# Three half-size raw weight tiles instead of one, and layer 1's embedding projection computed first

## The chip, the cores and the metric

One core of a Trainium2 chip runs the whole program in one launch. The metric is device microseconds of an execution, median of several. Five engines work side by side, each through its own queue in order: TensorE (PE in the profile; its weight loads are PEld), VectorE (DVE), ScalarE (ACT), GpSimd (POOL) and SyncE (SP), which here only issues DMAs.

## The reference, cut to what matters

Two layers on a residual stream of 512 tokens by 1024 columns, float32, then a final RMSNorm:

```python
for i in range(2):
    hn = rmsnorm(x, norm_g[i])
    x = x + (ab_mixer if i == 0 else fox_mixer)(hn, ...)      # hn @ w_in, heads, gate, @ w_out
    gate = sigmoid(rmsnorm(x, ple_norm_g[i]) @ w_ple_gate[i])
    x = x + gate * (p[i] @ w_ple_proj[i])                     # the per-layer embedding
return rmsnorm(x, final_g)
```

Layer 0's mixer has four gated-delta-rule heads (a short convolution on q, k, v; chunks of 64 tokens; a triangular inverse for each chunk) and four block-attention heads. Layer 1's mixer has eight heads with a forget gate (FoX). `p[i] @ w_ple_proj[i]` needs nothing of the residual stream: only `p` (512 by 256) and its weights (256 by 1024).

## The kernel before, in words

**Products.** A float32 product is made of three float32r products: each operand is split into a high part (its value rounded to float32r) and a low part (what is left), and high x high, low x high and high x low are summed in PSUM. One output tile of 128 x 512 (a "unit", `u` in the trace, or four rows of tokens, `vr`) takes 8 x 3 = 24 matmuls with 512 columns each.

**Weights.** Every weight matrix passes through one path (class `Weights`, lines 447 to 533). It is cut into pieces of 1024 x 512 (2 MB); a piece is loaded from DRAM into the tile `raw` (16 KB in each partition; there is one such tile) by two DMAs of 1 MB, one for each half of the rows. A piece is split in four chunks: a copy to `whi` (ACT, or DVE) and a subtraction to `wlo` (POOL, or DVE), each 128 x 1024; there are three `whi` and three `wlo` tiles. A chunk of a "cols" piece feeds one unit and holds all 8 row blocks, so it reads both halves of the piece; a chunk of a "rows" piece holds two row blocks, so it reads one half. `raw` is free for the next piece when the piece's fourth chunk is split. Of 23 pieces 19 are cols, 4 rows; two more chunks are `w_ple_proj[1]`.

**Order.** The order on every engine is written while the program is built, by the class `Plan` (lines 123 to 322). Each strand of work is a Python generator with a priority; `Plan` keeps an estimated time for each engine, tile and the DMA path (`bw`, line 177), and emits an instruction once its estimate says that its inputs are there at the present estimated time of PE. What is emitted is fixed: on the chip each engine runs its list in order and waits for the real event, however late it is. Where the estimate has nothing for PE for 0.2 us or more and a PSUM bank is free, it emits a matmul on a tile of ones, `idle` (line 296): a filler with no result.

**Tiles.** SBUF is cut by hand into pools: `t2` (2 KB tiles of 128 x 512, 55 of them: `NB2`), `t4` (4 KB, four), `raw`, `whi`, `wlo`, and the pair `bd` (8 KB each), which holds first `w_ple_proj[0]` and the gate weights, later the inverted blocks of the delta rule. PSUM banks are pools A (unit results) and B (all else).

**Around the change.** At the start `p[0]`, `w_ple_proj[0]` and `x` are loaded, layer 0's embedding product is computed (`ple_cols`, 48 matmuls, `pp`) and stored to DRAM (`ppd`), `x` is transposed and normalised, and the units of the delta rule's k follow, then the gate unit, q, the block attention's q, k, v, and v. The triangular inverse goes through DRAM (`xd`), from which 8 DMAs place 32 x 32 blocks in `bd` (lines 1182 to 1186); loads of `raw` are held from near the inverse's end until these are issued (line 484). `wy` (line 1188) multiplies with them (`t` in the trace). Layer 1's embedding product stands after the z units of FoX (lines 1588 to 1601), stays in eight `t2` tiles and is used in the last stage (`gate_row`, line 1662).

Of the kernel before, what the change touches and what calls it, by code (L numbers as in the profile page):

```python
# [122 lines left out]
class Plan:  # L123
# [34 lines left out]
    def emit(self, op):  # L158
# [12 lines left out]
        if op.eng == "PE":  # L171
            end += 0.18
        elif op.name == "dma_start":
            o = op.outs[0] if op.outs[0].space != bass.MemoryType.DRAM else op.ins[0]
            b = o.nbytes if not callable(o.nbytes) else o.nbytes()
            small = any(n.startswith(("kd", "ub", "xd", "graw", "vrow", "bd_", "qd", "gd", "Gb")) for n in op.w + op.r)
            self.bw = max(end + 0.7, self.bw) + max(b / 1e6 * 2.8, 0.6 if small else 0.2) + 1.5 * ("graw" in op.w[0])
            end = self.bw + 0.9
# [146 lines left out]
NB2, NBH = 55, 16  # L325
# [4 lines left out]
def kernel(  # L330
# [65 lines left out]
    bd = [gp.tile([P, GH * NT * P], F32, name=nm("bd"), tag="bd", bufs=2)]  # L396
    ple0 = bd[0].rearrange("p (k c) -> p k c", k=2)
    do(A.preload_act_table_set(LNEXP))
    for c in range(2):
        do(A.dma_start(ple0[:, :, c * 512:(c + 1) * 512],  # L400
                       w_ple_proj[0, :, c * 512:(c + 1) * 512].rearrange("(k q) c -> q k c", q=P)))
    do(A.dma_start(vrow1, norm_g.rearrange("i (f q) -> (i f) q", q=P)))
    xr = [plan.take("t4", "xr", (P, D)) for _ in range(NT)]
    for t in range(NT):
        for c in range(2):
            w = slice(c * S, (c + 1) * S)
            do(SP.dma_start(xr[t][:, w], x[0, t * P:(t + 1) * P, w]))
    do(A.dma_start(vrow[17:65], conv_w[0].rearrange("k (f q) -> (k f) q", q=P)))
# [31 lines left out]
    def gst_tile():  # L440
        return gp.tile([P, GH * NT, P], F32R, name=nm("gst"), tag="bd", bufs=2)[:, 0:KT, :]

    gst0 = gst_tile()
# [3 lines left out]
    class Weights:  # L447
# [13 lines left out]
        def cols(self, w, c0):  # L461

            self.add(self.views(w, c0), [(lambda r, j=j: r[:, :, j * P:(j + 1) * P], (KT, P)) for j in range(4)])

        def rows(self, w, c0):

            self.add(self.views(w, c0), [(lambda r, j=j: r[:, 2 * j:2 * j + 2, :], (2, 512)) for j in range(4)])

        def ple(self, w):
            self.add([w[:, c * 512:(c + 1) * 512].rearrange("(k q) c -> q k c", q=P) for c in range(2)],  # L470
                     [(lambda r, c=c: r[:, 2 * c:2 * c + 2, :], (2, 512)) for c in range(2)])
# [6 lines left out]
        def loads(self):  # L478
            for i, views in enumerate(self.pieces):
                if views is None:  # L480
                    self.loaded.append(ple0)
                    continue

                yield Wait(lambda: "inv3" not in flags or "bds" in flags)
                raw = yield Slot("raw", "raw", (P, KT, 512))
                n = views[0].shape[1]
                for k, view in enumerate(views):
                    yield SP.dma_start(raw[:, k * n:(k + 1) * n], view)
                self.loaded.append(raw)

        def splits(self):
            for i, (piece, f, (a, c)) in enumerate(self.chunks):
                yield Wait(lambda: len(self.loaded) > piece)
                raw = f(self.loaded[piece])
# [3 lines left out]
                yield copy(hi, raw, 0.8)  # L498
                w = [V.tensor_tensor(out=lo, in0=raw, in1=hi.bitcast(F32), op=ALU.subtract),
                     G.tensor_tensor(out=lo, in0=raw, in1=hi.bitcast(F32), op=ALU.subtract)]  # L500
                yield Any((w[0], 2.5 if far else 0.0), w[1])
# [34 lines left out]
    W.add(None, [(lambda r, c=c: r[:, :, c * 512:(c + 1) * 512], (2, 512)) for c in range(2)])  # L536
# [18 lines left out]
    W.ple(w_ple_proj[1])  # L555
# [14 lines left out]
    def later_loads():  # L570
        yield Wait(lambda: len(W.loaded) > 1)
# [380 lines left out]
    def spill(f):  # L952
        yield Wait(lambda: pps[f] is not None)
        yield SP.dma_start(ppd[f], pps[f])
        drop(pps[f])
        pps[f] = None
        spilled.add(f)

    ppd = dram.tile([KT, P, S], F32, name="ppd")
    spilled = set()  # L960
# [15 lines left out]

    ple_cols(pps)
    for f in range(KT):
        run(spill(f), 5)
# [176 lines left out]
    def inverses():  # L1156
# [25 lines left out]
        for k in (0, 1):  # L1182
            for bl in range(4):
                yield SP.dma_start(bds[k][bl * 32:(bl + 1) * 32, :, bl * 32:(bl + 1) * 32],
                                   xd[k, bl].rearrange("h t r c -> r (h t) c"))
        flags.add("bds")

    def wy(hh):
# [8 lines left out]
        yield flag("bds")  # L1197
        wq = yield Slot("t4", "wq", (P, NT, 4, 64))
        yield SP.dma_start(wq[:, :, 1:3, :], qd[hh].rearrange("p (t c i) -> p t c i", c=2, i=64))
        bdT, bd = (b[:, hh * NT:(hh + 1) * NT, :] for b in bds)  # L1200
# [28 lines left out]
        us[hh], wqs[hh], kds[hh] = u, wq, kdc  # L1229

# [81 lines left out]
    def blocks():  # L1312
        yield flag("gates")
        for k in range(2):
            bds.append(gp.tile([P, GH * NT, P], F32, name=nm("bd"), tag="bd", bufs=2))
            yield G.memset(bds[k], 0.0)
# [35 lines left out]
    run(gates(gate_unit(st["gst"], h)), -1)  # L1352
    delta()
# [4 lines left out]
    def ev_rows(ps, t, dst, parts, key):  # L1358
# [3 lines left out]
        if parts:  # L1362
            v = (None, t2("vhi", F32R), t2("vlo", F32R))
            yield A.activation(v[1], ps, AF.Copy, scale=s)
            yield V.scalar_tensor_tensor(out=v[2], in0=ps, scalar=s, in1=v[1].bitcast(F32), op0=ALU.mult, op1=ALU.subtract)
        else:
            v = (t2("vb"),)
# [48 lines left out]
    side_units(h, "k", range(4), 1.0, False, qkb)  # L1416
    for t, ps in enumerate(rowsV(h)):
# [9 lines left out]
    run(after(gens, lambda: [v[0] for v in vrows.values()]), 0)  # L1427
# [141 lines left out]
    for half in range(2):  # L1569
# [11 lines left out]
        run(after(gens[4 * half:], lambda half=half: [a for v in vrows2[half].values() for a in v if a is not None]), 0)  # L1581
    pT = []
    run(load_pT(1, None, pT.append, flag("z4")), 4)
# [4 lines left out]
    ppr = [None] * KT  # L1588
    for c in range(2):
        whi, wlo = W.get()  # L1590
        for t in range(NT):
            tt = slice(t * P, (t + 1) * P)
            pp = plan.slot("A", "pp")
            for k in range(2):
                until(lambda: len(pT) > k, "pT")
                for m, (a, b) in enumerate(((pT[k][0], whi), (pT[k][1], whi), (pT[k][0], wlo))):
                    plan.main(T.matmul(pp, lhsT=a[:, tt], rhs=b[:, k], start=(k + m == 0), stop=(k == 1 and m == 2)))
            run(keep(pp, ppr, c * 4 + t), 0)
        W.over((whi, wlo))
    for a in pT:  # L1600
        drop(*a)
# [11 lines left out]
    for a in y:  # L1613
        drop(*a)
    x3, h = x1, h3
# [7 lines left out]
    def late():  # L1623
# [6 lines left out]
        yield Wait(lambda: len(W.loaded) == len(W.pieces))  # L1630
        raw = yield Slot("raw", "raw", (P, KT, 512))
        for kc, view in enumerate(W.views(w_ple_gate[1], 512)):
            yield SP.dma_start(raw[:, kc * 4:(kc + 1) * 4], view)
        for kc in range(2):
            for k in range(4):
# [7 lines left out]
                yield copy(hi, raw[:, kc * 4 + k])  # L1643
                yield minus(lo, raw[:, kc * 4 + k], hi.bitcast(F32), 0.0)
                gw[kc * 4 + k] = (hi, lo)

    run(late(), -0.5)

    def gate_row(t, c, ps, ss, a, b, gt, before=None):
# [10 lines left out]
        if c == 1 and b == 512 and t != 2:  # L1660
            yield A.preload_act_table_set(LNEXP)
        yield V.tensor_tensor(out=gt[:, w], in0=gt[:, w], in1=ppr[c * 4 + t][:, w], op=ALU.mult)
        yield V.tensor_tensor(out=gt[:, w], in0=gt[:, w], in1=xps[:, w], op=ALU.add)
# [104 lines left out]
```

## Time and profile before

| | us |
|---|---|
| median of 3 runs | 742.52 (739.96 to 742.71) |
| the profiled execution | 739.63 |
| its span, first to last instruction | 737.9 |
| PE busy | 702.7 (95%) |
| DVE, ACT, POOL busy | 474.7, 341.1, 279.8 |
| granted TensorE clock, mean | 0.986 of 2.4 GHz |

PE is busy nearly throughout, and the fillers count as busy. What can be saved are the stretches where PE has no work, the fillers in front of them, and the stretches after them in which the clock is at its lower level. The table of 40 slices shows where; windows of a few us show how much.

### The profile page before, as it was taken

Reading aid. Unit: us, or ns where it says so; the run is one execution under the profiler, and the core shown is the slowest. Engines: PE = TensorE matmul, PEld = TensorE weight load, DVE = VectorE, ACT = ScalarE, POOL = GpSimd, SP = SyncE. Lnnn points to the kernel's source line nnn. Section 1 sums busy time; section 2 is a strip of 40 time slices with the busy share of each in tenths; the row PEclk is TensorE's granted clock in tenths of the full one; section 3 lists DMA queues with packets and bytes.
Section 4 is the critical chain, followed back from the end, with each engine's and each line's share of the span. In section 5 each row is a group of like instructions: output and inputs, shape, how many; then the busy total and the mean of one; then the engine's idle time right before and its main releaser. Section 6 shows DMA issues by size and latency. Waiting matters only on the chain.

```text
span 737.9 us, 9199 instructions
## 1 busy us (share of the span) xinstructions
PE 702.7 (95%) x3374; PEld 577.9 (78%) x3374; DVE 474.7 (64%) x805; ACT 341.1 (46%) x634; POOL 279.8 (38%) x222
## 2 busy tenths in 40 slices
PE   7999988999999999999998999989999799999995
PEld 4887876888788787778886888868888688888884
DVE  3768864966665678776896443546337466776684
ACT  4638842225774364634553422345224463433545
POOL 3435554426551223025322344342336322535320
PEclk9999999999999999999999999989999999999998
DMA  7752424443424023143554035310453203244303
GB/s 257 261 144 78 152 73 128 143 114 90 111 58 115 2 69 116 25 165 125 200 185 125 17 116 141 96 49 1 114 143 100 72 1 138 79 170 157 114 1 114
DMA packets 51782, 80.41 MB, mean 109 GB/s; under 512 B 11133, under 2 KB 14542, under 8 KB 51738
## 3 DMA queue, kind: packets, MB, share of 16 engines
q1 hardware_dynamic: 51064, 78.74, 34.5%
q10 hardware_dynamic: 674, 1.09, 0.5%
q8 instruction: 26, 0.43, 0.2%
q14 instruction: 18, 0.15, 0.1%
HBM read 68.53 MB, written 11.30 MB: 108 GB/s over the span
## 4 chain that ended last, share of the span: by engine, by line
PE 69%; DMA 13%; DVE 9%; ACT 3%; POOL 3%; issue 2%; SPq 1%; ACTq 0%; DVEq 0%; POOLq 0%
PE u L186 40%; PE vr L186 8%; DMA raw<-in_w_in_c_dram 6%; DMA raw<-in_w_in_ab_dram 4%; PE O L186 3%; PE pp L186 3%; PE fg L186 3%; POOL wlo L186 2%; PE S L186 2%; ACT whi L186 2%; PE PTp L186 2%; DVE gt L186 1%; DVE wlo L186 1%; DMA bd<-in_w_ple_proj_dram 1%; PE su L186 1%
## 5 line engine op out<-in xcount | busy, mean ns | idle before, releaser
L186 POOL TENSOR_TENSOR wlo<-raw,whi 128x1024 fp32r<-128x1024 f32 x74 | 186.5, 2526 | 360.0 <-ACT whi L186 280.6
L186 PE MATMUL u<-hhi,whi 128*128 128x512 f32 x480 | 190.7, 397 | 3.2 <-ACT whi L186 3.1
L186 PE MATMUL u<-hlo,whi 128*128 128x512 f32 x480 | 190.2, 396 | 0.0
L186 PE MATMUL u<-hhi,wlo 128*128 128x512 f32 x480 | 163.1, 397 | 0.1
L186 ACT ACTIVATE whi<-raw 128x1024 fp32r<-128x1024 f32 x84 | 87.3, 1054 | 117.7 <-DMA raw<-in_w_in_c_dram 49.5
L186 PEld LDWEIGHTS u<-hhi,whi 128*128 128x128 f32 x480 | 90.3, 188 | 22.1 <-ACT whi L186 3.5
L186 PEld LDWEIGHTS u<-hhi,wlo 128*128 128x128 f32 x480 | 89.7, 188 | 18.4 <-POOL wlo L186 0.6
L186 PEld LDWEIGHTS u<-hlo,whi 128*128 128x128 f32 x480 | 90.3, 188 | 17.3
L186 DVE TENSOR_TENSOR wlo<-raw,whi 128x1024 fp32r<-128x1024 f32 x20 | 36.9, 1844 | 24.8 <-ACT whi L186 24.8
L186 PE MATMUL u<-yhi,whi 128*128 128x512 f32 x128 | 50.2, 392 | 1.4 <-ACT whi L186 1.4
L186 PE MATMUL vr<-wlo,hhi 128*128 128x512 f32 x128 | 51.4, 401 | 0.0
L186 PE MATMUL vr<-whi,hlo 128*128 128x512 f32 x128 | 51.3, 401 | 0.0
L186 PE MATMUL vr<-whi,hhi 128*128 128x512 f32 x128 | 51.3, 401 | 0.0
L186 PE MATMUL u<-ylo,whi 128*128 128x512 f32 x128 | 50.0, 391 | 0.0
L186 ACT ACT_TABLE_LOAD x33 | 42.3, 1283 | 2.1 <-DVE cacc L186 0.8
L186 PE MATMUL u<-yhi,wlo 128*128 128x512 f32 x128 | 42.4, 391 | 0.7 <-POOL wlo L186 0.7
L186 ACT ACTIVATE hhi<-xres,vec 128x512 fp32r<-128x512 f32 x24 | 17.3, 724 | 44.1 <-DVE xres L186 44.0
L186 ACT ACTIVATE P<-P,nmx 128x128 f32<-128x128 f32 (+3 forms) x48 | 26.7, 557 | 12.6 <-DVE nmx L186 11.7
L186 DVE SCALAR_TENSOR_TENSOR cacc<-u,vec,cacc 128x509 f32<-128x509 f32 (+2 forms) x36 | 26.7, 744 | 7.0 <-ACT cacc L186 6.4
L186 PEld LDWEIGHTS u<-yhi,whi 128*128 128x128 f32 x128 | 24.1, 188 | 6.7 <-ACT whi L186 1.9
L186 PEld LDWEIGHTS u<-yhi,wlo 128*128 128x128 f32 x128 | 24.0, 188 | 6.0 <-POOL wlo L186 1.1
L186 PEld LDWEIGHTS vr<-whi,hlo 128*128 128x128 f32 x128 | 24.6, 193 | 4.9
(299 smaller groups left out, 1277.8 us busy)
## 6 DMA issues: line engine op xcount, KB each, us to landing
raw<-in_w_in_ab_dram SPq DMA_DIRECT2D x16, 1024.0 KB, 9.7
raw<-in_w_in_c_dram SPq DMA_DIRECT2D x16, 1024.0 KB, 7.0
raw<-in_w_ple_gate_dram SPq DMA_DIRECT2D x8, 1024.0 KB, 5.0
raw<-in_w_out_ab_dram SPq DMA_DIRECT2D x4, 1024.0 KB, 7.2
raw<-in_w_out_c_dram SPq DMA_DIRECT2D x4, 1024.0 KB, 6.5
xr<-in_x_dram SPq DMA_DIRECT2D x8, 256.0 KB, 5.6
x0d<-x SPq DMA_DIRECT2D x8, 256.0 KB, 8.0
ppd<-ppt SPq DMA_DIRECT2D x8, 256.0 KB, 4.1
```

The costliest lines, as they stand in the source:

```text
L186: return op.f(*op.a, **op.k)
```

## The change

- `raw` becomes three tiles of 8 KB, each for half a piece. A half is loaded as soon as one of the three is free. A chunk of a cols piece is split from its two halves by two copies and two subtractions of 128 x 512 each; a chunk of a rows piece still takes one of each, 128 x 1024.
- `Plan` counts 5.2 us for a MB of the two `w_in` matrices and 3.4 for other data, where it counted 2.8 for all.
- `t4` has 8 tiles, `t2` 51. The pair `bd` is gone: `w_ple_proj[0]`, the gate weights and the inverted blocks lie in `t4` tiles, the blocks in four (two heads each), filled by 16 DMAs of half the size. The values v of the block attention and the split v of FoX move from `t2` to `t4`.
- Layer 1's embedding product is computed right behind layer 0's (`ple_rows`), stored to DRAM (`ppd1`) and loaded back, eight tiles, in the last stage.

```diff
-            self.bw = max(end + 0.7, self.bw) + max(b / 1e6 * 2.8, 0.6 if small else 0.2) + ...
+            self.bw = max(end + 0.7, self.bw) + max(b / 1e6 * (5.2 if any("w_in" in n for n in op.r) else 3.4), 0.6 if small else 0.2) + ...
-NB2, NBH = 55, 16
+NB2, NBH = 51, 16
-    for pool, n in (("A", 4), ("B", 4), ("t2", NB2), ("th", NBH), ("t4", 4),
-                    ("raw", 1), ("whi", 3), ("wlo", 3)):
+    for pool, n in (("A", 4), ("B", 4), ("t2", NB2), ("th", NBH), ("t4", 8),
+                    ("raw", 3), ("whi", 3), ("wlo", 3)):
...
-                raw = yield Slot("raw", "raw", (P, KT, 512))
-                for k, view in enumerate(views):
-                    yield SP.dma_start(raw[:, k * n:(k + 1) * n], view)
-                self.loaded.append(raw)
+                for view in views:
+                    yield Wait(lambda: "inv3" not in flags or "bds" in flags)
+                    raw = yield Slot("raw", "raw", (P, 4, 512))
+                    yield SP.dma_start(raw[:, 0:view.shape[1]], view)
+                    self.loaded[i].append(raw)
...
-                yield copy(hi, raw, 0.8)
+                for h, k, w, o in parts:
+                    yield copy(hi[:, o, :], halves[h][:, k, w], 0.8)
+                for h, k, w, o in parts:
+                    ops = [e.tensor_tensor(out=lo[:, o, :], in0=halves[h][:, k, w], in1=hi[:, o, :].bitcast(F32),
+                                           op=ALU.subtract) for e in (V, G)]
+                    yield Any((ops[0], 2.5 if far else 0.0), ops[1])
...
-                if piece and (i + 1 == len(self.chunks) or self.chunks[i + 1][0] != piece):
-                    free(raw)
+                rest = {x[0] for q in self.chunks[i + 1:] if q[0] == piece for x in q[1]}
+                for h in {x[0] for x in parts} - rest:
+                    free(halves[h])
...
+    W.ple(w_ple_proj[1])          # now second in the list of pieces
...
     ple_cols(pps)
     for f in range(KT):
-        run(spill(f), 5)
+        run(spill(pps, f, ppd), 5)
+    ple_rows()
+    for f in range(KT):
+        run(spill(ppr, f, ppd1), 5)
...
-        for k in (0, 1):
-            for bl in range(4):
-                yield SP.dma_start(bds[k][...], xd[k, bl].rearrange("h t r c -> r (h t) c"))
+        for h0 in range(2):
+            yield Wait(lambda: len(bds) >= 2 * h0 + 2)
+            for k in (0, 1):
+                for bl in range(4):
+                    yield SP.dma_start(bds[2 * h0 + k][...], xd[k, bl, 2 * h0:2 * h0 + 2].rearrange("h t r c -> r (h t) c"))
+            flags.add(f"bds{h0}")
...
-    run(load_pT(1, None, pT.append, flag("z4")), 4)
...
+    for n in range(KT):
+        run(again(n), 3)          # ppr[n] back from ppd1
```

Because `Plan` writes the order anew, instructions move on every engine. Three places matter below.

ACT, in the first attentions of FoX: `whi` is a weight chunk, `PThi` the high part of transposed weights of attention that PE multiplies with v (`O`) next. Before:

```order
L186 ACTIVATE P_4084,sums_4024<-P_4084,nmx_4023 128x512
L186 ACTIVATE P_4092,sums_4063<-P_4092,nmx_4062 128x384
L186 ACTIVATE P_4060<-P_4060,rs_4096 128x384
L186 ACTIVATE whi_4101<-raw_4039 128x1024
L186 ACTIVATE P_4111,sums_4063<-P_4111,nmx_4062 128x512
L186 ACTIVATE PThi_4144<-PTp_4140 128x384
```

and in the change:

```order
L186 ACTIVATE whi_4317<-raw_4119 128x512
L186 ACTIVATE P_4306,sums_4274<-P_4306,nmx_4273 128x384
L186 ACTIVATE P_4316,sums_4298<-P_4316,nmx_4297 128x256
L186 ACTIVATE whi_4317<-raw_4189 128x512
L186 ACTIVATE P_4330,sums_4274<-P_4330,nmx_4273 128x512
L186 ACTIVATE P_4337,sums_4298<-P_4337,nmx_4297 128x384
L186 ACTIVATE P_4306<-P_4306,rs_4345 128x384
L186 ACTIVATE P_4360,sums_4298<-P_4360,nmx_4297 128x512
L186 ACTIVATE whi_4386<-raw_4119 128x512
L186 ACTIVATE PThi_4399<-PTp_4395 128x384
```

The copy of the next piece's first chunk stood two rows above the first `PThi`; it now stands in two parts nine and six rows above it, and the copy just above `PThi` reads a half that an earlier row has read already.

SP, at the end of the triangular inverse: `raw` are the weight loads, `xd` the inverse on its way through DRAM, `bd` its blocks, `wq` a load for the scan. Before:

```order
L186 DMA xd<-vb_650 64x1024
L186 DMA raw_1633<-in_w_in_ab_dram 128x4x512 x2
L186 DMA xd<-vbT_1602 64x1024
L186 DMA bd_1062<-xd 32x16x32 x4
L186 DMA bd_1064<-xd 32x16x32 x4
L186 DMA wq_1741<-qd 128x4x128
```

and in the change:

```order
L186 DMA raw_1784<-in_w_in_ab_dram 128x4x512
L186 DMA xd<-vb_761 64x1024
L186 DMA xd<-vbT_1793 64x1024
L186 DMA bd_1583<-xd 32x8x32 x4
L186 DMA bd_1585<-xd 32x8x32 x4
L186 DMA bd_1815<-xd 32x8x32 x4
L186 DMA bd_1817<-xd 32x8x32 x4
L186 DMA wq_1896<-qd 128x4x128
```

A load of 2 MB that stood between the two stores is now 1 MB ahead of them; eight block loads became sixteen, of which the first eight serve heads 0 and 1.

PE, between the k units of the delta rule with the gate unit (`tr` are transposes of k) and the q units. In the change:

```order
L186 MATMUL tr_791<-ident,cacc_737 128x128 x4
L186 MATMUL idle_812<-onesr 128x512
L186 MATMUL idle_816<-onesr 128x512
L186 MATMUL idle_822<-onesr 128x512
L186 MATMUL idle_824<-onesr 128x512
L186 MATMUL idle_826<-onesr 128x512
L186 MATMUL idle_828<-onesr 128x512
L186 MATMUL idle_831<-onesr 128x512
L186 MATMUL idle_834<-onesr 128x512
L186 MATMUL idle_836<-onesr 128x512
L186 MATMUL u_842<-hhi_373,whi_674 128x512
```

Before, there is no filler at this place; nine of them stand at another, between the fourth and the fifth unit of layer 0's output projection, where the change has none.

## Rows read from the trace of the kernel before

**Rows 1.** The page: busy time of PE; GB/s in 40 slices

```profile
PE 702.7 (95%) x3374; PEld 577.9 (78%) x3374; DVE 474.7 (64%) x805; ACT 341.1 (46%) x634; POOL 279.8 (38%) x222
...
GB/s 257 261 144 78 152 73 128 143 114 90 111 58 115 2 69 116 25 165 125 200 185 125 17 116 141 96 49 1 114 143 100 72 1 138 79 170 157 114 1 114
```

**Rows 2.** Windows: length, PE, PEld, DVE, ACT, POOL busy (x), clock, DMA, GB/s

```profile
92.00:100.00 8.00, 5.15 (x37) 4.68 (x36) 7.62 (x16) 4.69 (x10) 7.74 (x11) 1.00 0.05 8
116.00:122.00 6.00, 2.92 (x13) 2.10 (x12) 1.63 (x2) 2.12 (x3) 0.98 (x1) 1.00 0.55 189
294.00:300.00 6.00, 5.34 (x23) 4.06 (x23) 5.96 (x9) 5.96 (x10) 2.20 (x1) 1.00 0.00 0
314.00:322.00 8.00, 6.56 (x29) 5.07 (x28) 6.13 (x9) 3.68 (x4) 1.35 (x1) 1.00 0.67 252
390.00:400.00 10.00, 6.93 (x24) 5.17 (x23) 7.46 (x9) 4.90 (x6) 4.11 (x2) 0.83 0.11 32
480.00:492.00 12.00, 8.43 (x34) 6.83 (x33) 4.28 (x8) 3.91 (x9) 6.51 (x11) 0.72 0.27 69
566.00:582.00 16.00, 11.74 (x55) 9.54 (x54) 7.00 (x19) 6.16 (x15) 6.13 (x10) 0.89 0.50 157
```

**Rows 3.** Windows of the fillers alone: length, PE and PEld busy, clock

```profile
116.00:122.00 6.00, 0.86 (x3) 0.56 (x3) 1.00 0.55 189
294.00:300.00 6.00, 1.17 (x3) 0.56 (x3) 1.00 0.00 0
314.00:322.00 8.00, 2.23 (x9) 1.69 (x9) 1.00 0.67 252
566.00:582.00 16.00, 2.02 (x6) 1.13 (x6) 0.89 0.50 157
```

**Rows 4.** ACT in order of time: start, length, instruction [idle before <-releaser]

```profile
483.39 1.06 ACT L186 ACTIVATE whi<-raw 128x1024 fp32r<-128x1024 f32 x1 [7.09 <-DMA raw<-in_w_in_c_dram]
...
485.18 0.77 ACT L186 ACTIVATE PThi<-PTp 128x384 fp32r<-128x384 f32 x2
...
574.74 1.06 ACT L186 ACTIVATE whi<-raw 128x1024 fp32r<-128x1024 f32 x1 [5.22 <-DMA raw<-in_w_in_c_dram]
```

**Rows 5.** PE in order of time, in the first of these places

```profile
485.72 0.69 PE L186 MATMUL O<-PThi,vhi 128*128 128x384 f32 x1 [3.57 <-ACT PThi L186]
```

**Rows 6.** The chain that ended last: start, length, what

```profile
45.53 9.94 DMA raw<-in_w_in_ab_dram
...
417.66 43.52 PE u L186 x192
...
469.58 13.65 DMA raw<-in_w_in_c_dram
...
624.96 10.88 PE pp L186 x48
```

**Rows 7.** Instructions on raw: duration ns min/median/max; DMAs to landing

```profile
L186 ACT ACTIVATE whi<-raw x84: 1042/1053/1077, 26.9 to 678.5; 128x1024 fp32r<-128x1024 f32 x84
L186 POOL TENSOR_TENSOR wlo<-raw,whi x74: 2355/2402/3383, 28.0 to 685.5; 128x1024 fp32r<-128x1024 f32 x74
...
L186 ACT ACTIVATE gwhi<-raw x6: 616/618/634, 693.2 to 697.5; 128x512 fp32r<-128x512 f32 x6
...
L186 POOL TENSOR_TENSOR gwlo<-raw,gwhi x2: 1423/1581/1739, 697.1 to 698.5; 128x512 fp32r<-128x512 f32 x2
...
DMA to landing us min/median/max: 4.8/7.2/11.2
```

**Rows 8.** SP's issues in order of time, end of the inverse

```profile
177.84 0.51 SPq L186 DMA_DIRECT2D xd<-vbT  x1
178.45 12.94 SPq L186 DMA_DIRECT2D bd<-xd  x8
```

**Rows 9.** Instructions on bd: duration ns, first and last start us

```profile
L186 PE MATMUL t<-bd,kn x32: 271/275/276, 196.0 to 229.1; 128*128 128x128 f32 x32
```

**Rows 10.** PE in order of time, first matmul of the gate unit

```profile
54.70 0.39 PE L186 MATMUL gate<-hhi,gst 128*128 128x512 f32 x1
```

More of the change, by code (lines that the diff above doesn't have):

```diff
@@ L570, in later_loads @@
     def later_loads():
-        yield Wait(lambda: len(W.loaded) > 1)
+        yield Wait(lambda: len(W.loaded) > 1 and len(W.loaded[1]) == 2)
         yield load_gate("ab", w_in_ab[0], 1536)
@@ L975, in ple_cols, with spill, ple_rows @@
             drop(*a)
+    ppr = [None] * KT
+    ppd1 = dram.tile([KT, P, S], F32, name="ppd1")
+    def spill(dst, f, d):
+        yield Wait(lambda: dst[f] is not None)
+        yield SP.dma_start(d[f], dst[f])
+        drop(dst[f])
+        dst[f] = None
+    def ple_rows():
+        for c in range(2):
+            whi, wlo = W.get()
+            for t in range(NT):
+                tt = slice(t * P, (t + 1) * P)
+                pp = plan.slot("A", "pp")
+                for k in range(2):
+                    until(lambda: len(pT1) > k, "pT")
+                    for m, (a, b) in enumerate(((pT1[k][0], whi), (pT1[k][1], whi), (pT1[k][0], wlo))):
+                        plan.main(T.matmul(pp, lhsT=a[:, tt], rhs=b[:, k], start=(k + m == 0), stop=(k == 1 and m == 2)))
+                run(keep(pp, ppr, c * 4 + t), 0)
+            W.over((whi, wlo))
+        for a in pT1:
+            drop(*a)
+    pT1 = []
+    run(load_pT(1, prow1, pT1.append), -1)
     ple_cols(pps)
     for f in range(KT):
-        run(spill(f), 5)
+        run(spill(pps, f, ppd), 5)
+    ple_rows()
+    for f in range(KT):
+        run(spill(ppr, f, ppd1), 5)
     flags.add("pp")
@@ L1425, in after @@
         drop(*tiles())
-    run(after(gens, lambda: [v[0] for v in vrows.values()]), 0)
+    run(after(gens, lambda: vpair), 0)
     def gating(zs, order, oT, y, g):
@@ L1580 @@
         attend(qk, heads, lambda hh, i: (vrows2[hh // 4][i], slice((hh % 4) * P, (hh % 4 + 1) * P)), bias_c, oTc, 0.2, gens)
-        run(after(gens[4 * half:], lambda half=half: [a for v in vrows2[half].values() for a in v if a is not None]), 0)
-    pT = []
-    run(load_pT(1, None, pT.append, flag("z4")), 4)
+        run(after(gens[4 * half:], lambda half=half: [v[-1] for v in vrows2[half].values()]), 0)
     y = [None] * KT
@@ L1587, with again @@
         drop(*a)
[L1588 to L1601, printed above, removed]
+    def again(n):
+        r = yield Slot("t2", "ppr")
+        yield SP.dma_start(r, ppd1[n])
+        ppr[n] = r
     h3 = [None] * KT
@@ L1629, in late @@
             fg.append(fgt)
[L1630 to L1633, printed above, removed]
+        yield Wait(lambda: len(W.loaded) == len(W.pieces) and len(W.loaded[-1]) == 2)
+        raws = []
+        for view in W.views(w_ple_gate[1], 512):
+            raw = yield Slot("raw", "raw", (P, 4, 512))
+            yield SP.dma_start(raw, view)
+            raws.append(raw)
         for kc in range(2):
```

81 lines of the change are left out of this document (42 added, 39 removed).

## The prediction

> **What bounds the kernel now.** I read the page first: PE is busy 702.7 of 737.9 us [rows 1], so only time in which PE has nothing to do, or does fillers, can be saved. Next the windows around the holes in PE's work: idle time is a window's length less its PE time [rows 2], and the fillers in it are wasted too [rows 3]. The holes inside the run:
>
> | stretch | idle | fillers | together |
> |---|---|---|---|
> | 92 to 100 | 2.85 | 0 | 2.85 |
> | 116 to 122 | 3.08 | 0.86 | 3.94 |
> | 294 to 300 | 0.66 | 1.17 | 1.83 |
> | 314 to 322 | 1.44 | 2.23 | 3.67 |
> | 390 to 400 | 3.07 | 0 | 3.07 |
> | 480 to 492 | 3.57 | 0 | 3.57 |
> | 566 to 582 | 4.26 | 2.02 | 6.28 |
>
> In the window from 480 the mean granted clock is 0.72 [rows 2], so 0.56 of its 12 us, 6.7 us, ran at the lower level (1.2 GHz); 3.57 of these were the idle time, and the other 3.1 did half their work: 1.5 us more lost.
>
> Then I asked what ended the two FoX holes. ACT stood still for 7.09 us in front of a weight copy whose DMA had not landed, and for 5.22 us in front of another; the `PThi` that PE wanted came out right behind the first [rows 4], and PE's wait of 3.57 us ends there [rows 5]. The matmul and its operands were not late: a weight copy that nobody needed yet stood in front of them in ACT's list. The chain of waits names the loads: 9.94 us for a pair of w_in halves in layer 0, 13.65 us for one in layer 1 [rows 6]. The order was written with 2.8 us for a MB, 5.9 us for such a pair (2.1 million bytes). So the holes are late weight loads, seen directly at a unit or through an engine that waits for one in order.
>
> How late they must be: a unit costs 24 x 43.52/192 = 5.44 us [rows 6]. When a piece's fourth chunk is split, three chunks are left, 16.3 us, less the split of the fourth itself, 1.05 + 2.40 [rows 7]: 12.9 us. The next first chunk needs 0.94 for two issues, 9.94 for the pair, and 3.45 for its split: 14.3. Layer 0 is 1.4 us short, layer 1 5.1; pieces that land faster are not.
>
> **The change part by part.** *Three half tiles.* The first half of the next piece is now loaded ahead; only the second waits for the fourth split. A split made of halves takes 2 x 0.618 on ACT and 2 x 1.50 on POOL (middle of 1.42 and 1.58, the two forms of 128 x 512 [rows 7]), 4.2 us instead of 3.45. So 16.3 - 4.2 = 12.1 us are left, and 0.47 + half of 9.94 + 4.2 = 9.6 are needed, or 0.47 + half of 13.65 + 4.2 = 11.5: 2.5 and 0.6 us to spare. A rows piece gives back its first half two chunks earlier still. The four holes at weights (116, 294, 314, 566) go, as does the one from 480, where the ACT list now has the second half of the first chunk six rows above `PThi`: 3.94 + 1.83 + 3.67 + 6.28 + 3.57 + 1.5 = 20.8 us. The hole from 92 is a wait for `kn`, at the end of a chain on DVE; weight copies stand in DVE's list too, but no row says how much of it is load, 0 to 2.85, and I take 1.4. Together 22.2. The hole from 390 is the chain of sums behind the gated residual on a DVE busy 7.46 of 10 us; the change leaves it: 0.
>
> *What the new order puts in their place.* The list of PE has 47 fillers instead of 50: 13 before the first real product of the start (16 before), 4 around the two embedding products (5 in the first units before), 5 near the end (5), and within the run 9, 6, 3 and 7 (24 before). The nine at 314 cost 3.67 us, 0.41 each [rows 2, 3]; where the load was later than planned a filler cost more, but that is the part already taken away. 25 x 0.41 = 10.3 us. Two of the 24 before are at a place that I did not count as a gain, so 9.4 are new. Bounds: 25 x 0.23, the bare matmuls, 5.7, and the 1.3 us a filler of the place at 116, 33. The start gains 4 x 0.41 = 1.6.
>
> *Blocks of the inverse.* PE's list now runs into the first product with the blocks behind the v units. From the store of the inverse to that product it took 196.0 - 177.84 = 18.2 us [rows 8, 9], 12.94 of it for issuing eight loads. Only the first eight of sixteen must land, each half as large. If the issue goes by bytes, 6.5 us go, and 11.7 are left; PE has in its list, from the last rows of the inverse to the product, 45 matmuls of 512 columns and the six fillers, 51 x 0.227 = 11.6 us, and some transposes. Then nothing is late. If it goes by count, 18.2 - 11.6 = 6.6 us. I take 1, near the first, since an issue of a block load took 1.6 us where that of the store took 0.51: something that grows with its content sets it.
>
> *The moved product.* 48 matmuls, 10.88 us [rows 6], go from behind the z units to the start: PE pays them in both places, 0. At the start they are cover, since the DMA path there is full (257 and 261 GB/s in the first two slices [rows 1]). Up to the second half of the q weights 15 MB are asked for instead of some 12 (the product's inputs, 1.5, and its stores, 2): 15/0.259 = 58 us. PE was through the gate unit, 16 matmuls or 3.6 us, at 54.7 + 3.6 = 58.3 [rows 10], and now at some 58.3 + 10.9 = 69, so 11 us are to spare; if the rate fell to 200 GB/s the weights would come at 75, 6 us late. At the later place they covered a load; the half tile does that now. The loads back, 2 MB, stand in SP's queue ahead of the last stage and have most of a rows piece, 96 x 0.227 = 21.8 us, for 2.1/0.211 = 10: 0.
>
> *More, smaller instructions.* 0.8 us a cols chunk, hidden where a chunk is ahead; PE meets a chunk that is just being made at one or two places: 1 us. The two POOL rows are from one stage, so 0 to 5. `t2` with four tiles less has its price in the fillers, most of all in the nine before the q units.
>
> Sum: 739.63 - 22.2 + 9.4 - 1.6 + 1 + 1 = 727.2. The profiled execution lies 2.9 below the median, at the low end of the runs; I forecast 728, against the median of 742.5.
>
> **The rivals.** *The waits only move.* For: 25 fillers stand within the run as 24 did, and every estimate in the order was also wrong before. Then of 22.2 us only what is bare DMA lateness beyond the planned waits could go, 22.2 - 24 x 0.41 = 12.4, and as much comes back in other lists: about 740. Against: 2.8 us a MB was off by a factor of 1.7 to 2.3 from the rows, and 5.2 is not.
>
> *Block loads by count.* 6.6 us at the first product, where I took 1; the reload of k for the third head stands behind all sixteen in SP's queue and is issued 12.9 us later, of which I count half as covered: 727 + 5.6 + 6.5 = 739. Against: the 1.6 us of an issue, above.
>
> *Slower: a half lands no sooner than a pair.* If the 4.8 to 11.2 us of a landing [rows 7] are a wait that doesn't shrink with bytes, a cols piece needs 0.47 + 9.94 + 4.2 = 14.6 against 12.1: the holes stay, and each of the 19 cols pieces pays its 0.8 us longer split in full, 15 us: 739.6 + 15 = 755, or 748 where half of the pieces have slack. It decides from a landing of about 7.5 us for a half alone. Against: the pairs move 2 MB in 9.94 us, 211 GB/s, below the 261 that the path had at the start [rows 1].
>
> The Trainium skill, "DMA: Bandwidth & Descriptors", "Anatomy of one DMA", speaks for this rival in part: it fits a DMA with 2.0 us plus bytes over 436 GB/s, measured on GpSimd's own path. By it a half would take 0.65 of a pair, an estimate, the six cols pieces before the end of layer 1's mixer would each be 1.4 us short again, and the sum would be 735. The 13.65 us for 2 MB here are twice what the fit gives, so the trace puts more on the bytes than the fit does.
>
> *Slower: POOL becomes the bound.* It has 130 halves and 17 whole subtractions for 74: 130 x 1.50 + 17 x 2.40 = 236 us instead of 74 x 2.40 = 178 [rows 7]. A unit lasts 5.44 us, POOL's part of a chunk 3.0; it decides from 2.7 us a half. The longest whole one took 3.38 against a median of 2.40 [rows 7], so 2.1 a half at the worst: not reached. I put it with the rival above.
>
> The Trainium skill, "GPSIMD Engine Reference", "Specifications", says why it could be: GpSimd shares its SBUF interface with VectorE when that reads two SBUF inputs. More subtractions on POOL would then lengthen both; the spread from 2.36 to 3.38 us fits it.
>
> **How the numbers follow.** Forecast, 719 to 738: 0.71. Waits only move, about 740: 0.13. Blocks by count, 739: 0.04. Slower, 748 to 755: 0.12. The low end is every counted hole gone, 23.6, with bare fillers, 5.3 net, and the start: 739.6 - 23.6 + 5.3 - 1.6 = 719.7. The high end takes in the second and third case: 719 to 742. About 0.5% (3.7 us) can be told from no change with this kernel. Faster 0.75, same 0.12, slower 0.13.
>
> **What would show it.** Right: no ACT wait above 3 us for `raw` in front of `PThi`; PE idle under 1 us where the FoX attentions run; nine fillers before the q units with little idle behind them; halves landing in 5 to 7 us. Wrong: halves landing as late as the pairs; PE idle over 3 us before the first product with the blocks, or before the q units; POOL as the releaser of units; the clock down at a new place.

## The result and the profile after

The changed kernel takes 720.74 us (median of 4 runs, 719.83 to 721.73) against 742.62 us (739.96 to 744.93): a ratio of 0.9707, 95% interval 0.967 to 0.9744. The forecast was 728, with 719 to 742 as its range. The profiled execution took 719.85 us with a span of 718.1; by the terms of the prediction it should have taken 727.2.

The page's lines on PE, its clock and the DMA rate, in the change:

```profile
PE 699.5 (97%) x3371; PEld 573.4 (80%) x3371; DVE 461.0 (64%) x844; ACT 343.2 (48%) x677; POOL 315.9 (44%) x297
...
GB/s 260 163 361 188 63 148 157 152 86 72 117 118 30 61 58 50 128 159 174 84 155 197 111 4 116 151 142 1 118 20 128 146 2 176 17 185 288 8 1 118
```

Against [rows 1], PE's idle time fell from 35.2 us (737.9 less 702.7) to 18.6. That is 16.6 of the span's 19.8 us; 3.2 came out of the busy time.

The windows of the change, cut so that they cover its whole span; of those in which PE was busy all the time two are shown, one over layer 0's convolutions and one where the first FoX attentions run (columns as in [rows 2]):

```profile
0.00:20.00 20.00, 17.47 (x48) 9.99 (x49) 8.34 (x19) 5.25 (x9) 5.84 (x22) 1.00 0.80 273
...
60.00:90.00 30.00, 28.52 (x134) 22.76 (x133) 18.85 (x32) 18.67 (x53) 11.38 (x8) 1.00 0.29 88
90.00:130.00 40.00, 40.00 (x216) 34.36 (x216) 22.80 (x48) 23.79 (x69) 19.10 (x25) 1.00 0.51 156
...
180.00:240.00 60.00, 59.19 (x333) 46.98 (x332) 38.20 (x88) 39.10 (x80) 26.34 (x27) 1.00 0.32 80
240.00:300.00 60.00, 59.21 (x324) 47.57 (x323) 44.49 (x131) 29.69 (x70) 18.58 (x14) 1.00 0.30 88
...
390.00:405.00 15.00, 11.59 (x44) 8.82 (x43) 11.61 (x15) 7.21 (x9) 5.71 (x3) 0.89 0.39 112
...
480.00:492.00 12.00, 12.00 (x68) 10.01 (x66) 6.68 (x20) 6.06 (x14) 4.47 (x8) 1.00 0.11 34
492.00:582.00 90.00, 89.85 (x450) 75.35 (x448) 46.73 (x108) 40.54 (x94) 42.42 (x53) 1.00 0.29 83
...
700.00:718.00 18.00, 8.64 (x65) 8.00 (x63) 8.56 (x28) 9.41 (x16) 0.00 (x0) 0.88 0.32 117
```

All of PE's idle time is here: 2.5 us at the start, 9.4 at the end, 1.5 from 60, 0.8 and 0.8 from 180 and 240, 3.4 from 390 and 0.15 from 492. The holes of [rows 2] from 92, 116, 294, 314, 480 and 566 have no successor; the one from 390 is still there, at a clock of 0.89. Two new places are worth a look, from 69 and from 194. The fillers alone, at the four new places (columns as in [rows 3]):

```profile
69.00:76.00 7.00, 3.35 (x9) 1.60 (x9) 1.00 0.41 151
194.00:200.00 6.00, 2.06 (x6) 1.12 (x6) 1.00 0.56 125
496.00:500.00 4.00, 0.85 (x3) 0.56 (x3) 1.00 0.02 4
660.00:664.00 4.00, 1.78 (x7) 1.31 (x7) 1.00 1.06 389
```

With the idle time in these windows (1.48, 0.06, 0.15 and none) the 25 fillers stand for 4.83 + 2.12 + 1.00 + 1.78 = 9.7 us.

Instructions on raw in the change (columns as in [rows 7]):

```profile
L186 POOL TENSOR_TENSOR wlo<-raw,whi x147: 1268/1300/3248, 26.4 to 666.3; 128x512 fp32r<-128x512 f32 x130, 128x1024 fp32r<-128x1024 f32 x17
L186 ACT ACTIVATE whi<-raw x136: 612/623/1070, 25.3 to 665.2; 128x512 fp32r<-128x512 f32 x118, 128x1024 fp32r<-128x1024 f32 x18
L186 DVE CAST whi<-raw x34: 398/422/1512, 38.3 to 614.7; 128x512 fp32r<-128x512 f32 x34
...
DMA to landing us min/median/max: 4.9/7.8/11.4
```

A half copy costs what was expected, 0.62 us; a half subtraction on POOL 1.30 in place of 1.50. Landings did not get shorter: 7.8 us in the middle, where the DMAs of before, of the same 1 MB but issued in pairs, had 7.2 (first and second of a pair together).

ACT in order of time at the first `PThi` of the FoX attentions:

```profile
485.28 0.63 ACT L186 ACTIVATE whi<-raw 128x512 fp32r<-128x512 f32 x1 [1.27 <-PE vr L186]
486.82 0.49 ACT L186 ACTIVATE PThi<-PTp 128x384 fp32r<-128x384 f32 x1 [0.91 <-PE PTp L186]
```

The weight copy in front of `PThi` no longer waits for a load (7.09 us in [rows 4]) but for PE to give back a weight tile, and `PThi` waits for nothing but its own transposes.

The new place from 69. The landing of the second half of the q weights, a row on raw in a window that holds this one DMA, and then SP's issue of it and DVE where the first q chunk is copied, in order of time:

```profile
DMA to landing us min/median/max: 9.6/9.6/9.6
```

```profile
54.69 0.38 SPq L186 DMA_DIRECT2D raw<-in_w_in_ab_dram  x1
...
71.28 0.68 DVE L186 COPY row<-tr 128x512 f32<-128x512 f32 x1
71.88 0.53 DVE L186 TENSOR_SCALAR gy<-gy,gsgn,gbias 96x512 f32<-96x512 f32 x1
72.34 2.18 DVE L186 CAST whi<-raw 128x512 fp32r<-128x512 f32 x3
```

The weights lay there at 54.69 + 9.6 = 64.3 us, and their copy came at 72.3, because it stands in DVE's list behind work of the gate. No load is late here; the order is.

### The profile page after: what moved, and what is told of

It is laid out like the page before. It is cut to its first block, busy times and chain, and to the rows that moved or that the text cites. A ratio compares the mean times of both kernels' runs of the same rounds, so it can differ in the third digit from the quotient of the medians.

```text
span 718.1 us, 9435 instructions
## 1 busy us (share of the span) xinstructions
PE 699.5 (97%) x3371; PEld 573.4 (80%) x3371; DVE 461.0 (64%) x844; ACT 343.2 (48%) x677; POOL 315.9 (44%) x297
## 4 chain that ended last, share of the span: by engine, by line
PE 90%; DVE 6%; ACT 1%; issue 1%; POOL 0%; DVEq 0%; POOLq 0%; ACTq 0%
PE u L186 53%; PE vr L186 11%; PE O L186 3%; PE pp L186 3%; PE fg L186 3%; PE S L186 3%; PE idle L186 2%; PE PTp L186 2%; DVE gt L186 2%; DVE sq L186 1%; PE su L186 1%; PE gate L186 1%; PE t L186 1%; PE ws L186 1%; DVE xres L186 1%
## 5 line engine op out<-in xcount | busy, mean ns | idle before, releaser
L186 POOL TENSOR_TENSOR wlo<-raw,whi 128x512 fp32r<-128x512 f32 (+1 forms) x147 | 225.1, 1542 | 294.8 <-ACT whi L186 194.3
L186 ACT ACTIVATE whi<-raw 128x512 fp32r<-128x512 f32 (+1 forms) x136 | 88.2, 680 | 104.6 <-PE u L186 64.0
L186 PEld LDWEIGHTS vr<-whi,hhi 128*128 128x128 f32 x128 | 24.3, 190 | 6.3 <-DVE gt L186 1.4
L186 PEld LDWEIGHTS u<-ylo,whi 128*128 128x128 f32 x128 | 24.0, 188 | 5.5 <-DVE ylo L186 0.5
L186 PEld LDWEIGHTS vr<-wlo,hhi 128*128 128x128 f32 x128 | 24.3, 190 | 4.7
```

The lines of the kernel that those rows point to most:

```text
L186: return op.f(*op.a, **op.k)
```

## The experiments

Theory A: the holes were late weight loads, and they close because a third half tile lets a load start ahead. Rival B: they close because the planner's price of a MB is now right, so that copies no longer stand in front of ready work. Beside these two: what the moved product and the fillers cost by themselves. Each was timed in five rounds beside the kernel before, which took 744.0 us in the runs with e1 to e4, 744.0 with e5 to e8, 742.2 with e9 to e12; between these groups the ratios compare better than the times.

| run | what | us | ratio to before, 95% |
|---|---|---|---|
| e1 | before, new prices alone | 745.24 | 0.9986 to 1.0036 |
| e6 | change, raw one tile of 16 KB | 746.01 | 1.001 to 1.0045 |
| e3 | change, two halves | 724.33 | 0.9695 to 0.9767 |
| | the change | 720.74 | 0.967 to 0.9744 |
| e9 | change, no fillers inside | 718.46 | 0.9652 to 0.9693 |
| e4 | change, product late again | 716.29 | 0.9584 to 0.9655 |
| e2 | change, old price 2.8 | 714.48 | 0.9562 to 0.9632 |
| e5 | both taken back: tiles alone | 714.73 | 0.9579 to 0.9633 |
| e8 | e5, loads by quarters | 712.72 | 0.9546 to 0.96 |
| e10 | e5 at 2.0, two halves | 718.46 | 0.9645 to 0.9693 |
| e7 | e5 at 2.0 | 709.84 | 0.9516 to 0.9566 |
| e11 | e5 at 1.0 | 709.97 | 0.9536 to 0.9581 |
| e12 | e8 at 2.0 | 710.46 | 0.9543 to 0.9583 |

**e1, the prices alone**, in the kernel before:

```diff
-            ... + max(b / 1e6 * 2.8, 0.6 if small else 0.2) + ...
+            ... + max(b / 1e6 * (5.2 if any("w_in" in n for n in op.r) else 3.4), 0.6 if small else 0.2) + ...
```

> The kernel before with only its planner's price of a MB changed (5.2 for w_in and 3.4 for the rest in place of 2.8); raw stays one tile of 16 KB, the product stays late. Its list has 119 fillers against 50. Theory A, the load ahead into a third half tile is what closed the waits: the holes in front of PThi go (11 to 13 us), but the loads stay as late, and the 69 fillers more cost 0.23 to 0.41 us each, 16 to 28: 742.6 - 12 + 16 to 28 = 745 to 760, or no better than 735 where a filler stands in time that was lost before. Theory B, the price of a MB was the fault, since with the right one the copies stand behind the work that is ready: 720 to 728.

745.24 us, no difference from before: B falls as the whole cause. The page of e1:

```profile
PE 718.6 (97%) x3443; PEld 587.8 (79%) x3443; DVE 475.2 (64%) x818; ACT 327.6 (44%) x615; POOL 282.1 (38%) x222
```

PE is idle 25.5 of 744.1 us, 9.7 less than before, and busy 15.9 more: the waits are now written down as fillers (119 for 50). A longer estimate of a late load does not make it earlier.

**e3, two halves**, everything else as in the change:

```diff
-                    ("raw", 3), ("whi", 3), ("wlo", 3)):
+                    ("raw", 2), ("whi", 3), ("wlo", 3)):
```

> The changed kernel with two half tiles for raw in place of three, everything else equal (prices 5.2 and 3.4, product early). Its list has 93 fillers against 47. Theory A: the gain of the third tile goes: 46 fillers more at 0.23 to 0.41, 11 to 19 us: 732 to 740. Theory B (the price did it): 720 to 725, since the fillers only stand in slack.

724.33 us, where A had 732 to 740. In this form A falls too: at these prices the third half is worth no more than some 4 us, which the intervals do not part from nothing. The 46 fillers more add 8.9 us to PE's busy time (708.4 of a span of 722.7 us), and its idle time is 4.3 us shorter. Since e1 had ruled out the price, the amended theory was that the same 16 KB do better as two tiles than as one, because each half is given back, and loaded again, by itself.

**e6, raw one tile of 16 KB** in the changed kernel, loaded by two DMAs:

```diff
-                    ("raw", 3), ("whi", 3), ("wlo", 3)):
+                    ("raw", 1), ("whi", 3), ("wlo", 3)):
...
-                    raw = yield Slot("raw", "raw", (P, 4, 512))
+                whole = yield Slot("raw", "raw", (P, KT, 512))
...
+                    raw = whole[:, 4 * k:4 * k + 4]
```

and the whole is freed behind the last chunk of its piece.

> The changed kernel (price 5.2, product early, pool of 4 KB tiles, splits by halves) with raw as one tile of 16 KB, loaded by two DMAs and given back as one. It has 169 fillers against 93 of the kernel with two half tiles and 47 of the changed one. If it is the tile given back by halves that closed the waits: 742 to 760, at least as slow as the kernel before with the new prices (745). If it is the rest of the change (blocks by pairs of heads, pool, shorter instructions): within 4 us of the kernel with two half tiles, 724.

746.01 us, as slow as e1. So two half tiles beat one tile of the same 16 KB by 21.7 us (e3), and the rest of the change, at these prices, is worth nothing: the first part of the amended theory holds. Its reason is another matter. Here is a place where e6 loses time, ahead of layer 1's v units, whose weights are a rows piece, so that the first two chunks need the first half alone. The landings of a pair in e6, from a window with these two DMAs alone, and then SP's issue, the ACT copies, POOL around its first subtraction and PE's fillers and wait, in order of time:

```profile
DMA to landing us min/median/max: 7.6/10.2/12.9
```

```profile
470.20 0.92 SPq L186 DMA_DIRECT2D raw<-in_w_in_c_dram  x2
...
478.99 1.99 ACT L186 ACTIVATE whi<-raw 128x1024 fp32r<-128x1024 f32 x2
...
482.97 1.33 PE L186 MATMUL idle<-onesr 128*128 128x512 f32 x5
...
484.48 0.73 POOL L186 COPY biasc<-biasc 128x128 f32<-128x128 f32 x1
485.17 3.31 POOL L186 TENSOR_TENSOR wlo<-raw,whi 128x1024 fp32r<-128x1024 f32 x1
...
488.53 0.50 PE L186 MATMUL vr<-wlo,hhi 128*128 128x512 f32 x1 [2.38 <-POOL wlo L186]
```

In e3, SP's three issues there, the ACT copies and PE at the same matmul:

```profile
454.98 0.37 SPq L186 DMA_DIRECT2D raw<-in_w_in_c_dram  x1
...
456.88 0.37 SPq L186 DMA_DIRECT2D raw<-in_w_in_c_dram  x1
...
463.04 2.01 ACT L186 ACTIVATE whi<-raw 128x1024 fp32r<-128x1024 f32 x2 [2.62 <-DMA raw<-in_w_in_c_dram]
...
467.74 0.37 SPq L186 DMA_DIRECT2D raw<-in_w_in_c_dram  x1
...
470.19 0.39 PE L186 MATMUL vr<-wlo,hhi 128*128 128x512 f32 x1
```

In e3 the issues are spread: the halves of a piece at 455 and 457, and the first half of the next one 10.9 us behind, as soon as two chunks are split. The landings are no shorter there (10.4 us for the second, 7.5 for the third). So loads do start earlier where halves are given back by themselves.

At cols pieces e6 has late loads in fact: a pair issued at 125.1 landed at 136.6, amid 16 fillers from 135.0 to 138.9. But at the place shown no late load held PE. The first half had landed at 470.20 + 7.6 = 477.8, 5.2 us before PE ran out of work, and its copies were done by 481.0; the subtraction that PE wanted stood in POOL's list behind other work until 485.17. PE ran 11 fillers here and stood 2.38 us. `Plan` keeps one time for a tile, and for the tile of 16 KB that is the landing of its second half, so it also writes the split of the first half too late. Half tiles thus change two things: when a load starts, and from when `Plan` counts a half as there. How the 21.7 us are shared between them no run shows.

**e2, the old price** in the changed kernel:

```diff
-            ... + max(b / 1e6 * (5.2 if any("w_in" in n for n in op.r) else 3.4), 0.6 if small else 0.2) + ...
+            ... + max(b / 1e6 * 2.8, 0.6 if small else 0.2) + ...
```

> The changed kernel with the old price of 2.8 us a MB; three half tiles, product early. Its list has 38 fillers against 47. Theory A: loads are a half ahead and no unit waits more; 719 to 726, with at most one wait of ACT over 3 us ahead of PThi. Theory B: copies stand in ACT's and DVE's lists ahead of what is ready, holes of 3 to 6 us come back at three or four places: 732 to 740.

714.48 us, against B, and less than A's 719: faster than the change by some 1.1% (the intervals do not touch). The first q copies stand on ACT there:

```profile
61.30 1.68 ACT L186 ACTIVATE whi<-raw 128x512 fp32r<-128x512 f32 x3 [1.21 <-DMA raw<-in_w_in_ab_dram]
```

and over the window from 62 to 76 PE is busy all 14 us. The copy waits 1.21 us for its load, and nobody is held up; in the change it came 8 us after its load and the q units were late.

**e4, the product late again**, its stores and reloads gone:

```diff
-    W.ple(w_ple_proj[1])
     B0 = 1544
...
+    W.ple(w_ple_proj[1])
     for c0 in (0, 512):
         W.cols(w_out_c[0], c0)
...
-    ple_rows()
-    for f in range(KT):
-        run(spill(ppr, f, ppd1), 5)
...
+    run(load_pT(1, None, pT1.append, flag("z4")), 4)
...
     z_units(h, tuple(range(KT)), "f", lambda f: oTc.get(f), y)
...
+    ple_rows()
...
-    for n in range(KT):
-        run(again(n), 3)
```

> The changed kernel with layer 1's projection back behind layer 1's z units, without the stores and loads of its result. Its list has 53 fillers against 47, 12 of them at the first units of layer 0 in place of 4, one at the q units in place of nine. If the move is worth nothing by itself, as predicted: 720 to 725. If the product at the start is cover for the weight loads and its late place costs a wait there: 727 to 732. If the move costs time (its 2 MB of stores and 1.5 MB of loads put the q weights late): 714 to 718.

716.29 us, the third guess: with the new price the move costs some 0.9%. Its reason is another than the one given there, since the q weights had landed 8 us before their copy. **e5, the tiles alone** (e2 and e4 together):

> The changed kernel with both other edits taken back: the price of a MB is 2.8 again, and layer 1's projection stands behind its z units. Left are the half tiles and the pool of 4 KB tiles. If the two edits cost time each by itself (6.3 and 4.5 us by the runs before): 709 to 711. If both costs are the same one, the nine fillers and the late copy ahead of the q units: 713 to 715.

714.73 us, as fast as e2. So the two costs are one: at 2.8 us a MB the product's place is worth nothing, and at 5.2 the planner believes the q weights to be later still behind the product's stores, and puts their copy back.

**e7 and e11, lower prices** with the tiles alone (e7; e11 has 1.0 there):

```diff
-            ... + max(b / 1e6 * 2.8, 0.6 if small else 0.2) + ...
+            ... + max(b / 1e6 * 2.0, 0.6 if small else 0.2) + ...
```

> As the kernel with the tiles alone, with 2.0 us a MB. 30 fillers against 42, none ahead of layer 0's first units. If a price below what a load takes is harmless while loads stand a half ahead: the same as at 2.8 or 1 to 2 us less. If copies get in the way of ready work again: 3 to 8 us more, with ACT waits for raw over 3 us.

> The kernel with the tiles alone at 1.0 us a MB, 26 fillers. If the price does harm only when it is above what a load takes: 708 to 711, as at 2.0. If copies come to stand too early in ACT's and DVE's lists: 713 or more, with waits of ACT for raw over 3 us.

709.84 and 709.97 us, 5 less than at 2.8, more than guessed. A price below what a load takes did no harm here, with three half tiles; e7 beats the kernel before by 4.6% and the change by 1.7%, and is the best here. Its page:

```profile
PE 691.5 (98%) x3354; PEld 571.9 (81%) x3354; DVE 455.6 (64%) x827; ACT 343.1 (48%) x684; POOL 325.8 (46%) x305
```

**e10, two halves at 2.0**, in e7 the edit of e3:

> The kernel with the tiles alone at 2.0 us a MB, with two half tiles for raw in place of three; 22 fillers against 30. With 5.2 us a MB the third half was worth 3.6 us. If the third tile is needed because the loads are late in fact: 713 to 718 against 709.8 with three. If it only kept the planner from writing waits down: 709 to 711.

718.46 us against 709.84: at this price the third half is worth some 8.6 us (9.5 by the ratios). Two of PE's waits in e10 lie at the hole that all versions have around 380 to 400:

```profile
380.25 0.79 PE L186 MATMUL vr<-whi,hhi 128*128 128x512 f32 x1 [3.53 <-DVE gt L186]
...
400.50 0.87 PE L186 MATMUL rrps<-ident,rstd 128*128 128x128 f32 x4 [2.70 <-DVE rstd L186]
```

PE waits for DVE there, 6.2 us in these two, where e7 has two waits of 2.6 us together at this hole; what stands in DVE's way, and where the rest of the 8.6 us lies, was not followed further.

**e9, no fillers inside the run** of the change:

```diff
-            if self.warm is not None and asleep >= 0.2 and ...
+            if self.warm is not None and (t0 < 45.0 or t0 > 690.0) and asleep >= 0.2 and ...
```

> The changed kernel without the 25 fillers inside the run (9 ahead of the q units, 6 ahead of the products with the blocks, 3 in the first FoX attentions, 7 in the last stage); those at the start and the five near the end stay. By the prediction's term a filler is worth 0.41 us of waste, bounds 0.23 to 1.3; if the fillers push the work behind them out by their own length: 711 to 715. If PE would only have stood idle in their place, for the copy that stands late in its engine's list: 719 to 722. If the clock falls where PE now rests: 722 or more.

718.46 us, 2.3 less, just below the second guess; the intervals overlap. PE in windows that hold the four places, without their fillers (columns as in [rows 2]), and its wait in the second of them:

```profile
69.00:76.00 7.00, 6.20 (x36) 5.05 (x35) 5.64 (x9) 6.69 (x23) 2.61 (x2) 1.00 0.40 151
194.00:200.00 6.00, 3.64 (x11) 2.00 (x10) 3.21 (x7) 5.35 (x8) 3.52 (x5) 0.75 0.45 106
496.00:500.00 4.00, 3.16 (x16) 2.42 (x15) 3.54 (x8) 3.56 (x8) 1.31 (x2) 1.00 0.00 0
655.00:665.00 10.00, 9.54 (x43) 7.55 (x42) 9.93 (x11) 5.86 (x9) 7.18 (x5) 1.00 0.84 314
```

```profile
197.40 0.48 PE L186 MATMUL PTp<-ident,P 128*128 128x128 f32 x1 [2.36 <-DVE P L186]
```

PE is idle 0.80 + 2.36 + 0.84 + 0.46 = 4.5 us there, where fillers and idle time took 9.7. So about half of that marked waits that remain, the largest for the softmax rows ahead of the products with the blocks; the other half, most of it at the q units, went with the fillers. The whole gains only 2.3 us, and the clock has a part in that: behind the wait of 2.36 us, in a window where the fillers had kept it at 1.00, it is 0.75 in the mean, half of the window at the lower level (1.2 GHz).

**e8 and e12, loads by quarters** (each half by two DMAs of 512 KB, in e5 and in e7):

```diff
-                    yield SP.dma_start(raw[:, 0:view.shape[1]], view)
+                    m = view.shape[1] // 2
+                    for k in range(2):
+                        yield SP.dma_start(raw[:, k * m:(k + 1) * m], view[:, k * m:(k + 1) * m])
```

> As the kernel with the tiles alone, with every half loaded by two DMAs of 512 KB. In the changed kernel a half alone lands in 4.9 to 11.4 us, 7.8 in the middle. If the bytes set that, the second of two quarters lands when the half did and the time is the same within 2 us. If a part of it is a wait of each DMA by itself, quarters that are issued together land 0.5 us later at most, or sooner when two run beside each other: the same to 2 us less. If issues count (0.37 to 0.4 us each): 1 to 3 us more.

> The kernel with the tiles alone at 2.0 us a MB, each half loaded by two DMAs of 512 KB. A quarter alone landed in 3.9 us where a half alone took 5.0 to 5.1. If the 2 us between the two kernels at 2.8 came from earlier landings: 707 to 709. If they came from another list: 709 to 711.

712.72 us, 2.0 less than e5 (the runs of the two don't overlap), and 710.46, no less than e7. By the second guess on e12 those 2 us came from another list rather than from earlier landings.

## Why the prediction was right, and where its steps were not

**The holes go: right, and in part for the reason given.** 20.8 us were counted at weights and in front of `PThi`; none of these holes is left, and e6 against e3 shows that raw in halves is what closes most of them, at 21.7 us; the third tile, on which I built, adds some 4 at 5.2 us a MB (not clear of noise) and 8.6 at 2.0 (e10). That halves let loads start earlier is shown; that all of the gain comes from it is not, since the halves have times of their own in `Plan` as well (e6). The hole from 92 went whole (2.85, taken as 1.4), the one from 390 stayed, as forecast.

**Why they go: wrong in the working.** I let a half land in half of a pair's time (5 us, 5 to 7 as the sign to look for). Halves took 7.8 in the middle, among other DMAs; by themselves 5.1 to 5.9 (below). So the condition of the rival on landings, 7.5 for a half alone, was not met to the letter, but halves came as late as the pairs did, a sign named for being wrong, and nothing of what that rival foretold came. Its sum and mine had the same fault: both put the second half's landing and a split of 4.2 us in a row. The first half's copy and subtraction need not wait for the second half, and a half subtraction took 1.30: after the last landing 0.62 + 1.30 = 1.92 us are left, so 0.47 + 7.8 + 1.9 = 10.2 us of 16.3 - 3.2 (the fourth chunk's split: 0.62 + 2 x 1.30) = 13.1. That is worked out from the rows above; no run took it apart.

The Trainium skill ("DMA: Bandwidth & Descriptors", "Anatomy of one DMA") fits a DMA with 2.0 us plus bytes over 436 GB/s, by which a half takes 0.65 of a pair, an estimate. From w_out and w_ple_gate the trace agrees: halves that found the path empty landed in 5.1 us, 0.6 to 0.7 of the 7.3 to 8.5 that the second DMA of a pair from w_out took in e6. From w_in, on which the sums were built, 5.9 (below) stand against 9.0 to 13.0 there, 0.45 to 0.65, which does not decide between the page and my half. The page's 735 us failed on the same fault in the sum.

**"2.8 us a MB was off, 5.2 is not": the step that failed.** I took the new price as part of the cure. By e1 it cures nothing, by e2 and e4 it is what makes the new hole at the q units, and of the prices tried 2.0 and 1.0 were best (e7, e11). That the forecast held with it is in part luck: this step cost 6.3 us against e2, and the sum was too long elsewhere. The DMA path was not full either at the 257 to 261 GB/s on which I built: the change moved 361 in a slice of its start. The q weights were there at 64.3 us, and the moved product did not make them late.

**The start**, taken as a gain of 1.6 us. PE comes to the gate unit here:

```profile
64.62 0.39 PE L186 MATMUL gate<-hhi,gst 128*128 128x512 f32 x1
```

With the 10.88 us of the moved product [rows 6] on top of [rows 10] it would have been 65.58: 1.0 gained.

**New fillers.** 25 at 0.41 make 10.3; with the idle time beside them they stand for 9.7. The size was right; by e9 about half of it are waits that would be there anyway.

**POOL as the bound** did not come: busy 315.9 of 718.1 us, and a half subtraction is quicker than taken.

**Blocks.** Wrong reason, small number. In the change sixteen issues took less time than eight had:

```profile
188.90 7.73 SPq L186 DMA_DIRECT2D bd<-xd  x16
```

That is 0.48 us each with the gaps between (0.33 to 0.45 by instruction) for half the content, against 0.30 to 3.24 in [rows 8]. The long ones before stood behind 2 MB of weights that SP had issued from 176.87 on. That the content does not set it is shown by e1, which issues the same eight as before, but 11 us behind its weights, at 0.34 to 0.49 us each:

```profile
161.25 0.94 SPq L186 DMA_DIRECT2D raw<-in_w_in_ab_dram  x2
...
172.22 4.06 SPq L186 DMA_DIRECT2D bd<-xd  x8
```

So what stands ahead in the queue fits as the reason. From store to product it took 200.7 - 186.9 = 13.8 us in place of 18.2. In front of the product stand the six fillers, which the term of the fillers holds already, and 0.06 us of idle time where 1 was taken.

**The difference in the sum**, 727.2 less 719.85 = 7.4 us: 1.45 is the rest of the hole from 92, 1 is the cost of smaller instructions, of which no row shows any, 0.9 the blocks, 0.6 the fillers, less 0.6 at the start. About 4 are left. PE's fillers alone, before and in the change, each over the whole span (columns as in [rows 3]):

```profile
0.00:738.00 738.00, 18.35 (x50) 10.26 (x50) 0.99 0.35 109
0.00:718.20 718.20, 20.93 (x47) 9.91 (x47) 0.99 0.38 118
```

Without them PE is busy 702.7 - 18.35 = 684.4 us before and 699.5 - 20.93 = 678.6 in the change, 5.8 less for the same 3324 matmuls (a filler overlaps its neighbours, so this is rough). The mean granted clock went from 0.986 of 737.9 us to 0.994 of 718.1, which is 20.7 us at the lower level before and 8.6 now, and fits matmuls that got shorter. Only 1.5 us of lost work was counted for it, at one of the three holes of [rows 2] in which the clock was down; the other 4.3 are about what is left.

## What to carry over

Where a unit waits for a load, look at the tile that it goes into: when it came free, which is when the load could start, and from when the planner counts it as there. The same 16 KB as two tiles instead of one were worth 21.7 us, a longer estimate of the lateness nothing. In an order that is written ahead, an estimate that was too late cost more here than one that was too early, once there was a buffer ahead: a copy that is put behind other work stays there when its data comes sooner, while one that comes early waits a little on an engine with slack. An edit that comes out at nothing should be tried with its neighbours taken back, since the move cost 0.9% beside one price and nothing beside another.

## What was not expected of the hardware

DMAs of weights that found the path empty, though others were issued behind them, fit a fixed part and a rate. The landing of one half of 1 MB in the change (issued at 654.8), the change's DMA rate from 654.5 to 660 in 40 slices, and the landing of a quarter of 512 KB in e8 (issued at 335.0):

```profile
DMA to landing us min/median/max: 5.1/5.1/5.1
```

```profile
GB/s 0 0 0 0 0 0 0 0 0 74 45 0 0 0 45 238 298 372 417 387 417 417 402 417 402 417 387 417 432 402 402 402 417 387 417 417 402 402 402 387
```

```profile
DMA to landing us min/median/max: 3.9/3.9/3.9
```

1.2 us for 0.524 million bytes are 437 GB/s, and some 2.7 us are left that do not shrink. Two landings, each read to 0.1 us, are a thin base; while the bytes move, the row shows 372 to 432 GB/s. The fit of the Trainium skill, named above, has 2.0 us and 436 GB/s for GpSimd's path. SP's queue agrees with the rate as far as this goes, and its fixed part here is 0.7 longer. Loads from w_in are slower by themselves: 5.9 us for the half issued at 403.2.

DVE's copies of a half, 0.42 us in the middle, took up to 1.51 in the change; the long ones lie beside a POOL instruction with two inputs, as the third of those at 72.34 does, whose POOL neighbour starts at 72.83. POOL's own half subtractions did not lengthen beside such a copy as much (1.40 for the one at 72.83, where most take 1.27 to 1.36). But 31 of the 130 took 1.6 us or more, and each of these lies beside a VectorE instruction with two inputs, as here, where VectorE's is long too (`gt<-gt,ppr` of the same shape took 0.68 us at 361.40, with no POOL work beside it):

```profile
363.36 1.77 POOL L186 TENSOR_TENSOR wlo<-raw,whi 128x512 fp32r<-128x512 f32 x1 [2.42 <-ACT whi L186]
363.89 1.79 DVE L186 TENSOR_TENSOR xres<-xres,gt 128x512 f32<-128x512 f32 x1
```
